# One VectorE operation in place of eight on GpSimd, a third PSUM bank for linear products, and the logarithm ahead of the exponentials, in a hybrid decoder step

## The chip, the cores and the metric

The kernel runs on one core of one Trainium2 chip. A core has engines that each work through a list of instructions of their own: TensorE (PE in the profile, with its weight loads as PEld), VectorE (DVE), ScalarE (ACT), GpSimd (POOL) and SyncE (SP), which here issues nearly all transfers. TensorE writes its products to PSUM, which this kernel uses as eight banks of 128 partitions x 512 float32 numbers; ACT and DVE read the banks out. Everything else lies in SBUF or in the chip's main memory. The metric is the device time of one execution in microseconds (us), lower is better.

## The reference

One inference step of a one-layer decoder. A group of 512 prompt tokens and a group of 8 samples with 4 new tokens each (32 tokens) go through the same weights, with model width 1024.

```python
h = _rms_norm(x, pre_mix_g)
proj = h @ w_in                       # conv value | conv gate | r | k | v | LoRA inputs | merge gates
o_a = conformer branch(proj)          # sigmoid gate, causal conv of width 31, LayerNorm, silu, w_conv_out
...
kk = k * k_k
kk = kk * lax.rsqrt(jnp.maximum(jnp.sum(kk * kk, axis=-1, keepdims=True), 1e-24))
decay = jnp.exp(-jnp.exp(w_log)); a = jax.nn.sigmoid(iclr_base + l_iclr @ w_iclr_up)
# per token and head, with a 64x64 state s:
sk = jnp.einsum('bhvk,bhk->bhv', s, kk_t)
s = s * w_t[:, :, None, :] - sk[..., None] * (kk_t * a_t)[:, :, None, :] + v_t[..., None] * k_t[:, :, None, :]
y_t = jnp.einsum('bhvk,bhk->bhv', s, r_t)
...
o_b = ((group_norm(y) + bonus) * g) @ w_rwkv_out
m = (sigmoid(gA) * o_a + sigmoid(gB) * o_b) @ w_out
x = x + _rms_norm(m, post_mix_g)
x = x + _rms_norm(jnp.square(jax.nn.relu(_rms_norm(x, pre_ffn_g) @ w_ff_up)) @ w_ff_down, post_ffn_g)
```

Outputs are the new hidden rows and the states (convolution, token shift, and the 64x64 state `s` of each of the 16 heads) of prompt and samples.

## The kernel before

Activations lie transposed: 128 channels in the partitions, the 544 tokens (512 prompt, 32 samples) in the free dimension, in two halves of 272 (or 276, with the 8 shift rows). Each float32 matrix product of a weight block is made of three products of a high and a low part (`whi`, `wlo`, `xhi`, `xlo`), L152 in `part_steps`: eight blocks of the contraction x 3 = 24 matmuls a half. Each half takes a PSUM bank with the tag `lin` from the pool `pl`, which has two; when its 24 matmuls are done, ACT or DVE or both read it out (the "evacuation"). Weights come in blocks of 128x1024: `wraw` loads one, `wsplit` makes `whi` by a copy (on ACT or POOL, L140) and `wlo` by a subtraction on DVE (L141), with two buffers for each.

The first stage, to about 830 us, computes `w_in` and the mixer for eight pairs of heads (`p` = 0 to 7). The main loop at the end of the first stage traces the work of a pair in this order: `chain(p - 1)`, which steps through the eight prompt chunks of the pair before; the block `K`; `rates(p)`; `front(p)` with the blocks `R` and `W`; `value(p)`; `tokens(p)`; the inverse of a triangular matrix for each chunk (`inverse`, 15 small steps on DVE, then products with the tag `pb`); `sample(p)`; `groupnorm(p - 1)`; and `fill`, which adds linear blocks of the gates. The `yield` statements in these generators are run through and have no effect on the order, save for the marks "R" and "front". The framework places the instructions of each engine in a fixed list when the program is built. It takes those that are ready first by the order of tracing, where its own estimate of durations says when something is ready, and gives a tile a buffer of its tag once a buffer is free. Within a list nothing overtakes. Convolution work (L292 on DVE) carries a lower priority and fills in.

PSUM in this stage: `lin` two banks, `pb` two (one tile of two banks), and one each of `aux`, `ch`, `yt` and `ax`, from the pool `qc`. `ax` serves the LoRA products and the sum over the key in `rates`, the bonus in `value`, and the group norm's products. `aux` serves `sample`. `yt` holds four chunks of the chain's output.

What the change touches:

- `rates(p)`: `sg` (decay) and `a` come from sigmoids on ACT (L458). Three exponentials of the running sum of `sg` give `pin`, `epp` and `eps` (L468 to L472). Then the key's norm: square (L477), sum by a product (L480), Ln (L481), Exp (L485). Functions of different tables need a table load on ACT (L228); `tact` (L232) keeps all such functions in the order in which they are traced.
- `sample(p)`: a small system for the 32 sample tokens in `aux`. At its end `uv` holds values in the partitions, and the new state of the eight samples is a product of `zbt` with `ux`, in which each sample's columns hold `uv` masked to that sample (L751 to L759); DVE adds the old state (L760), POOL scales it by `epS` (L762), SP stores it (L763).
- `groupnorm(p)`: mean and variance by products (L781, L784), and the gate's LoRA product (L793), in `ax`.

The second stage (from about 830 us) makes the output products and the feed-forward layers from pools of its own, `pl2` with three banks and `ql` with two, and hardly anything else.

Of the kernel before, what the change touches and what calls it, by code (L numbers as in the profile page):

```python
# [8 lines left out]
F32 = mybir.dt.float32  # L9
F32R = mybir.dt.float32r  # L10
AF = mybir.ActivationFunctionType
ALU = mybir.AluOpType
MULT, ADD, SUB = ALU.mult, ALU.add, ALU.subtract
# [4 lines left out]
NB = 8  # L18
TS = 4
N2 = T + NB * TS  # L20
N1 = N2 + NB
NPAIR = 8
C = 64
# [5 lines left out]
CDEC = math.exp(-0.5)  # L29
# [4 lines left out]
PE, ACT, DVE, SP, POOL = (getattr(mybir.EngineType, e) for e in ("PE", "Activation", "DVE", "SP", "Pool"))  # L34
# [28 lines left out]
def hybrid_step(ctx: ExitStack, tc: tile.TileContext, xT, hist, s0, win, wco, wro, wo, wup, wdn, lora,  # L63
                vecs, convw, cst, yo, convo, shifto, wkvp, wkvs):
    nc = tc.nc
    PSUM = bass.MemoryType.PSUM
    act = nc.scalar.activation
    tt, stt, ts = nc.vector.tensor_tensor, nc.vector.scalar_tensor_tensor, nc.vector.tensor_scalar
# [7 lines left out]
    pg = ctx.enter_context(tc.tile_pool(name="pg", bufs=16))  # L76
    cv = ctx.enter_context(tc.tile_pool(name="cv", bufs=1))
    wp = ctx.enter_context(tc.tile_pool(name="wp", bufs=WB))
    pl = ctx.enter_context(tc.tile_pool(name="pl", bufs=2, space=PSUM))
    dr = ctx.enter_context(tc.tile_pool(name="dr", bufs=1, space=bass.MemoryType.DRAM))  # L80

    vt = cp.tile([128, NV], F32, name="vt")
# [10 lines left out]
    rms_eps, ln_eps, gn_eps, kk_neg, kk_eps, kk_log = (epst[:, i:i + 1] for i in range(6))  # L93
# [20 lines left out]
    def con(name):  # L114
        o = COFF[name]
        return cs[:, o:o + dict(CONSTS)[name]]
# [115 lines left out]
    def tact(name, *args, **kw):  # L232

        with tables(name):
            lastact[0] = act(*args, **kw)
        return lastact[0]

    SIG, LN, EXP, LNEXP = "sigmoid_and_others", "natural_log", "exp_and_others", "natural_log_exp_and_others"
# [3 lines left out]
    with tc.tile_pool(name="p0", bufs=1) as p0, tc.tile_pool(name="q0", bufs=1, space=PSUM) as q0:  # L242
        start = tables(LNEXP)
# [8 lines left out]
        rs, rt = (p0.tile([128, N1], F32, name=n) for n in ("rs", "rt"))  # L252
        hfs = [p0.tile([128, N1], F32, name=f"hf{k}") for k in range(KT)]
        with start:
            for s, (o, m) in enumerate(S1):
                q = slice(o, o + m)
                ps = q0.tile([128, 512], F32, name=f"ss{s}")
# [21 lines left out]
    def sv(t):  # L279

        return t[:, T:N2].rearrange("p (b t) -> p b t", t=TS)
# [52 lines left out]
    with ExitStack() as c1:  # L334
# [101 lines left out]
        def sum_steps(lhsT, x, evac, pool, tag):  # L436
            for s, (o, m) in enumerate(S2):
                ps = pool.tile([128, 512], F32, name=tag, tag=tag)[:, 0:m]
                nc.tensor.matmul(ps, lhsT, x[:, o:o + m], start=True, stop=True)  # L439
                evac(s, ps, o, m)  # L440
                yield ACT

        def rates(p):

            lraw = page("k2")[:, 0:128]
            nc.sync.dma_start(lraw, lora[p, :, 0:128])
            yield (ACT,)
            glu_sig()
            yield
            for i in range(2):  # L450
                split_hl(up[0][H[i], i, :], up[1][H[i], i, :], lraw[H[i]])
            yield
            ap_ = p1.tile([128, 2 * N2], F32, name="ap", tag="ap")
            sg, a, pin = page("sg"), ap_[:, 0:N2], ap_[:, N2:2 * N2]
            for i, (d, b) in enumerate(((sg, "decay_base"), (a, "iclr_base"))):
                for s, (o, m) in enumerate(S2):
                    yield from part_steps([(up[0][:, i], up[1][:, i])], [ld], s, o, m,
                                          lambda s, ps, o, m: tact(SIG, d[:, o:o + m], ps, AF.Sigmoid, bias=vec(b, p)),  # L458
                                          qc, "ax")
            nc.vector.tensor_tensor_scan(sg[:, 0:N2], con("scan"), sg[:, 0:N2], 0.0, MULT, ADD)  # L460
            ep = p1.tile([128, NC * (C + 1) + 40], F32, name="ep")
            e0 = NC * (C + 1)
            epp = ep[:, 0:e0].rearrange("p (c t) -> p c t", c=NC)
            eps = ep[:, e0:e0 + 40].rearrange("p (b f) -> p b f", f=TS + 1)
            nc.vector.memset(epp[:, :, 0:1], 1.0)
            nc.vector.memset(eps[:, :, 0:1], 1.0)
            yield ACT
            tact(EXP, pin[:, 0:N2], sg[:, 0:N2], AF.Exp, scale=CDEC)  # L468
            yield (ACT,)
            tact(EXP, epp[:, :, 1:C + 1], ch3(sg), AF.Exp, scale=-CDEC)  # L470
            yield (ACT,)
            tact(EXP, eps[:, :, 1:TS + 1], sv(sg), AF.Exp, scale=-CDEC)  # L472
            yield ("K", p, ACT)

            k = pgs["k", p]
            k2 = page("k2")
            act(k2[:, 0:N2], k[:, 0:N2], AF.Square, scale=vec("k_k", p))  # L477
            yield
            rs = page("rs")
            yield from sum_steps(con("blk1"), k2, lambda s, ps, o, m: act(rs[:, o:o + m], ps, AF.Relu, bias=kk_neg), qc, "ax")  # L480
            tact(LN, rs[:, 0:N2], rs[:, 0:N2], AF.Ln, scale=2.0 ** 20, bias=kk_eps)  # L481
            yield (ACT,)
            kp = page("k2")
            act(kp[:, 0:N2], a[:, 0:N2], AF.Identity, scale=vec("k_a", p), bias=oka[:, p:p + 1])
            tact(EXP, rs[:, 0:N2], rs[:, 0:N2], AF.Exp, scale=-0.5, bias=kk_log)  # L485
            yield DVE
            st2(kp[:, 0:N2], k[:, 0:N2], kp[:, 0:N2], MULT)
            st2(a[:, 0:N2], a[:, 0:N2], pin[:, 0:N2], MULT)
            yield (DVE,)
            kk = page("kk")  # L490
            stt(out=kk[:, 0:N2], in0=k[:, 0:N2], scalar=vec("k_k", p), in1=rs[:, 0:N2], op0=MULT, op1=MULT)
            yield DVE
            pgs["pre"] = ep, epp, eps, a, pin, kk, kp
# [66 lines left out]
        def value(p):  # L560

            f, v, rk = fs[p], pgs["v", p], pgs["k", p]
            bon = f["bon"] = p2.tile([128, N2], F32, name="bon")
            yield from sum_steps(con("blk1"), rk, lambda s, ps, o, m: tt(out=bon[:, o:o + m], in0=ps,
                                                                       in1=v[:, 64 + o:64 + o + m], op=MULT),
                                 qc, "ax")
            if p:
                yield ("smp", p - 1, ACT)
            nc.scalar.copy(vpad[:, :, 32:64], v[:, 64 + T:64 + N2].unsqueeze(1).to_broadcast([128, 2, 32]))
            yield  # L570
# [121 lines left out]
        def sample(p):  # L692
# [55 lines left out]
            for i in range(2):  # L748
                tt(out=y[H[i], :], in0=xy[0:64, 320 + 32 * i:352 + 32 * i],
                   in1=xc[0:64, 64 * i + 32:64 * i + 64], op=ADD)  # L750
            for b in range(0, NB, 4):  # L751
                ux = p1.tile([128, 4, 64], F32, name="ux")
                for e in range(4):
                    nc.gpsimd.tensor_scalar(ux[:, e, :], uv[:, 0:64], con("bmask")[:, b + e:b + e + 1], None, MULT)  # L754
                yield
                if b == 0:
                    ps = qc.tile([128, NB, 64], F32, name="aux", tag="aux")
                nc.tensor.matmul(ps[:, b:b + 4].rearrange("p b v -> p (b v)"), zbt, ux.rearrange("p b v -> p (b v)"),
                                 start=True, stop=True)  # L759
            tt(out=st, in0=ps, in1=st, op=ADD)  # L760
            for b in range(NB):
                nc.gpsimd.tensor_scalar(st[:, b, :], st[:, b, :], f["epS"][:, b:b + 1], None, MULT)  # L762
# [3 lines left out]
        def groupnorm(p):  # L766
            f, y = fs[p], pgs["y", p]
            nc.scalar.copy(y[:, T:N2], ys[p])
            yc, sq = page("t0", cv), page("t1", cv)
            lraw = yc[:, 0:128]  # L770
            nc.sync.dma_start(lraw, lora[p, :, 128:256])
            lhi = p1.tile([128, 128], F32R, name="lhi")
            llo = p1.tile([128, 128], F32R, name="llo")
            yield ACT
            split_hl(lhi, llo, lraw)
            yield

            def cevac(s, ps, o, m):
                act(sq[:, o:o + m], ps, AF.Square)
                nc.scalar.copy(yc[:, o:o + m], ps)  # L780
            yield from sum_steps(con("cent"), y, cevac, qc, "ax")  # L781
            yield
            rs = sq
            yield from sum_steps(con("blkm"), sq,  # L784
                                 lambda s, ps, o, m: tact(LNEXP, rs[:, o:o + m], ps, AF.Ln, bias=gn_eps), qc, "ax")
            tact(LNEXP, rs[:, 0:N2], rs[:, 0:N2], AF.Exp, scale=-0.5)
            yield DVE
            o = yc[:, 0:N2]
            stt(out=o, in0=o, scalar=vec("lnx_g", p), in1=rs[:, 0:N2], op0=MULT, op1=MULT)
            yield DVE  # L790
            stt(out=o, in0=f["bon"], scalar=vec("lnx_b", p), in1=o, op0=ADD, op1=ADD)
            yield
            for s, (oo, m) in enumerate(S2):  # L793
                yield from part_steps([(lhi, llo)], [lg], s, oo, m,
                                      lambda s, ps, oo, m: tt(out=yc[:, oo:oo + m], in0=ps, in1=yc[:, oo:oo + m], op=MULT),
                                      qc, "ax")
            nc.sync.dma_start(o_dr[p], o)

        def block(b, p):
# [110 lines left out]
    for j in range(KT):  # L910
        o = page("o")
# [235 lines left out]
```

## Time and profile before

| | us |
|---|---|
| median of 3 runs | 1377.77 (1374.94 to 1379.05) |
| the profiled execution | 1375.78 |
| its span, first to last instruction | 1373.6 |
| mean granted TensorE clock | 0.963 |

"Busy" is the time in which an engine executed something; matmuls overlap each other, so PE busy is not PE at its peak. The windows give this per stretch of time. A wait is an idle time of an engine before an instruction, with the instruction of another engine that ended it ("PE lin L152 <- DVE r L379": PE stood before a linear product until DVE's evacuation at line 379 was done). "issue" is idle time that the profile ties to nothing. In a timeline, a row gives start, duration, engine, line and tiles (output<-inputs), and in brackets the idle time ahead of it. In groups of instructions the columns are count, busy us, mean ns of one, and the idle us before them.

### The profile page before, as it was taken

The numbers are of one execution on the slowest core, as the hardware profiler recorded it, in microseconds if no ns is written. First come the engines' busy times: TensorE is split into PE (matmuls) and PEld (weight loads), VectorE is DVE, ScalarE is ACT, GpSimd is POOL, SyncE is SP. The second block draws the span as 40 slices with busy tenths as digits, with TensorE's granted clock in tenths as the row PEclk, the third lists the DMA queues.
The fourth block names the chain that finished last, engine by engine and source line by source line (L and its number), as shares of the span: only waits on it lengthen the run. The fifth ranks groups of instructions, "written<-read, shape, count | busy, mean of one in ns | idle before, by whom it ended". The sixth has DMA issues, their size and how long they took to land.

```text
span 1373.6 us, 23314 instructions
## 1 busy us (share of the span) xinstructions
PE 1266.3 (92%) x9170; PEld 1192.4 (87%) x9170; DVE 811.7 (59%) x1521; ACT 672.5 (49%) x1595; POOL 245.5 (18%) x376
## 2 busy tenths in 40 slices
PE   6978998989899798898889999999999999999996
PEld 5968887787787778778788999999999999999995
DVE  5798768653876768767657746566833221333345
ACT  7452746657374563743733438245755322555231
POOL 2125333142433225232230120000000000000000
PEclk9999998999999899999999999999999999999998
DMA  5312111111201212012121565245023222322331
GB/s 183 99 46 90 45 47 48 30 65 34 77 18 42 77 34 64 31 42 87 33 65 44 177 215 173 89 128 177 28 62 93 86 84 83 101 81 91 93 93 66
DMA packets 46333, 110.61 MB, mean 81 GB/s; under 512 B 7184, under 2 KB 17680, under 8 KB 46224
## 3 DMA queue, kind: packets, MB, share of 16 engines
q1 hardware_dynamic: 46080, 109.05, 25.0%
q8 instruction: 72, 1.18, 0.3%
q14 instruction: 37, 0.30, 0.1%
q10 hardware_dynamic: 144, 0.07, 0.0%
HBM read 94.79 MB, written 14.32 MB: 79 GB/s over the span
## 4 chain that ended last, share of the span: by engine, by line
PE 64%; ACT 9%; DVE 7%; POOL 4%; issue 3%; DMA 1%; SPq 0%; DVEq 0%; POOLq 0%; ACTq 0%
PE lin L152 47%; PE pb L608 4%; ACT SV L679 2%; PE ax L439 2%; POOL ux L754 2%; POOL st L762 2%; PE ch L664 2%; PE ch L675 2%; ACT SV L673 2%; PE ch L671 1%; PE ax L152 1%; DVE c L292 1%; PE yt L668 1%; PE pb L544 1%; PE ch L666 1%
## 5 line engine op out<-in xcount | busy, mean ns | idle before, releaser
L152 PE MATMUL lin<-xh,whi 128*128 128x272 f32 (+1 forms) x2096 | 623.8, 298 | 22.1 <-DVE r L379 10.3
L152 PE MATMUL lin<-xh,wlo 128*128 128x272 f32 (+1 forms) x2096 | 624.5, 298 | 0.6 <-DVE wlo L141 0.6
L152 PE MATMUL lin<-xl,whi 128*128 128x272 f32 (+1 forms) x2096 | 622.4, 297 | 0.1
L152 PEld LDWEIGHTS lin<-xh,whi 128*128 128x128 f32 x2096 | 405.4, 194 | 25.7 <-issue 13.6
L152 PEld LDWEIGHTS lin<-xh,wlo 128*128 128x128 f32 x2096 | 405.0, 193 | 1.9 <-DVE wlo L141 0.8
L152 PEld LDWEIGHTS lin<-xl,whi 128*128 128x128 f32 x2096 | 404.6, 193 | 1.3 <-DVE xl L174 0.3
L141 DVE TENSOR_TENSOR wlo<-raw,whi 128x1024 fp32r<-128x1024 f32 x131 | 160.6, 1226 | 211.1 <-ACT whi L140 175.9
L292 DVE SCALAR_TENSOR_TENSOR c<-u,cw,c 128x512 f32<-128x512 f32 x240 | 187.0, 779 | 8.9 <-issue 4.8
L140 ACT CAST whi<-raw 128x1024 fp32r<-128x1024 f32 x76 | 79.7, 1049 | 122.4 <-PE lin L152 118.8
L140 POOL CAST whi<-raw 128x1024 fp32r<-128x1024 f32 x55 | 65.3, 1187 | 314.6 <-issue 166.0
L152 PE MATMUL lin<-xh,wl 128*128 128x272 f32 x240 | 69.4, 289 | 0.0
L152 PE MATMUL lin<-xl,wh 128*128 128x272 f32 x240 | 69.3, 289 | 0.0
L152 PE MATMUL lin<-xh,wh 128*128 128x272 f32 x240 | 69.2, 288 | 0.0
L1006 DVE TENSOR_TENSOR xl<-ff,xh 128x272 fp32r<-128x272 f32 x64 | 28.3, 442 | 55.9 <-ACT ff L1005 55.9
L228 ACT ACT_TABLE_LOAD x45 | 57.7, 1283 | 2.0 <-PEq L1129 1.2
L679 ACT ACTIVATE SV<-ch,pc 64x64 f32<-64x64 f32 x128 | 39.5, 309 | 20.4 <-PE ch L675 19.1
L673 ACT ACTIVATE SV<-ch 64x64 f32<-64x64 f32 x128 | 27.9, 218 | 37.0 <-PE ch L671 35.1
L152 PEld LDWEIGHTS lin<-xh,wh 128*128 128x128 f32 x240 | 45.2, 188 | 0.1
L152 PEld LDWEIGHTS lin<-xh,wl 128*128 128x128 f32 x240 | 45.2, 188 | 0.1
L152 PEld LDWEIGHTS lin<-xl,wh 128*128 128x128 f32 x240 | 45.1, 188 | 0.1
L754 POOL TENSOR_SCALAR ux<-uv,cs 128x64 f32<-128x64 f32 x64 | 33.9, 549 | 51.6 <-DVE uv L745 47.2
L762 POOL TENSOR_SCALAR st<-st,epS 128x64 f32<-128x64 f32 x64 | 40.0, 648 | 11.4 <-DVE rt L588 5.8
(275 smaller groups left out, 1894.1 us busy)
## 6 DMA issues: line engine op xcount, KB each, us to landing
raw<-win SPq DMA_DIRECT2D x58, 512.0 KB, 3.6
raw<-wup SPq DMA_DIRECT2D x32, 512.0 KB, 3.6
raw<-wdn SPq DMA_DIRECT2D x32, 512.0 KB, 3.6
g_dr<-g SPq DMA_DIRECT2D x16, 272.0 KB, 2.3
raw<-wro SPq DMA_DIRECT2D x8, 512.0 KB, 3.9
raw<-wco SPq DMA_DIRECT2D x8, 512.0 KB, 3.6
raw<-wo SPq DMA_DIRECT2D x8, 512.0 KB, 3.6
x<-xT SPq DMA_DIRECT2D x8, 276.0 KB, 5.0
```

Source lines behind the costliest of these rows:

```text
L140: upper(hi, r)
L141: tt(out=lo, in0=r, in1=hi.bitcast(F32), op=SUB)
L152: nc.tensor.matmul(ps, a, b[:, o:o + m], start=k == 0 and i == 0, stop=k == n - 1 and i == 2)
L228: lastact[0] = nc.scalar.preload_act_table_set(name)
L292: stt(out=c[:, 0:T], in0=u[:, t:t + T], scalar=w[:, t:t + 1], in1=c[:, 0:T], op0=MULT, op1=ADD)
L439: nc.tensor.matmul(ps, lhsT, x[:, o:o + m], start=True, stop=True)
L608: nc.tensor.matmul(ps[:, c, :], lhsT(c), rhs[:, c, :], start=True, stop=True)
L673: nc.scalar.mul(SV[H[i], c, i, :], ch[H[i], 2, B[i]], -1.0)
L679: nc.scalar.mul(SV[H[i], c + 1, i, :], ch[H[i], 1, B[i]], pc[H[i], c:c + 1])
L754: nc.gpsimd.tensor_scalar(ux[:, e, :], uv[:, 0:64], con("bmask")[:, b + e:b + e + 1], None, MULT)
L762: nc.gpsimd.tensor_scalar(st[:, b, :], st[:, b, :], f["epS"][:, b:b + 1], None, MULT)
L1006: tt(out=lo[:, q], in0=t[:, q], in1=hi[:, q].bitcast(F32), op=SUB)
```

## The change

Four edits.

1. In `sample`, the eight POOL operations that masked `uv` for each sample, in two groups of four with a product of 256 columns each, become one `tensor_tensor` on DVE with both operands broadcast (128 x 8 x 64 = 512 columns) and one product of 512 columns.
2. The pool `pl` for linear products has three banks in place of two.
3. The bank `ax` is gone: `rates` and `value` now take theirs from `aux`, which `sample` uses too, and `groupnorm` takes its from `yt`, which the chain uses.
4. In `rates`, the three exponentials of the decay stand behind the Ln and the Exp of the key's norm.

```diff
-    pl = ctx.enter_context(tc.tile_pool(name="pl", bufs=2, space=PSUM))
+    pl = ctx.enter_context(tc.tile_pool(name="pl", bufs=3, space=PSUM))
...
                                           lambda s, ps, o, m: tact(SIG, d[:, o:o + m], ps, AF.Sigmoid, bias=vec(b, p)),
-                                          qc, "ax")
+                                          qc, "aux")
...
-            yield ACT
-            tact(EXP, pin[:, 0:N2], sg[:, 0:N2], AF.Exp, scale=CDEC)
-            yield (ACT,)
-            tact(EXP, epp[:, :, 1:C + 1], ch3(sg), AF.Exp, scale=-CDEC)
-            yield (ACT,)
-            tact(EXP, eps[:, :, 1:TS + 1], sv(sg), AF.Exp, scale=-CDEC)
-            yield ("K", p, ACT)
...
-            yield from sum_steps(con("blk1"), k2, lambda s, ps, o, m: act(rs[:, o:o + m], ps, AF.Relu, bias=kk_neg), qc, "ax")
+            yield from sum_steps(con("blk1"), k2, lambda s, ps, o, m: act(rs[:, o:o + m], ps, AF.Relu, bias=kk_neg), qc, "aux")
             tact(LN, rs[:, 0:N2], rs[:, 0:N2], AF.Ln, scale=2.0 ** 20, bias=kk_eps)
...
             tact(EXP, rs[:, 0:N2], rs[:, 0:N2], AF.Exp, scale=-0.5, bias=kk_log)
+            tact(EXP, pin[:, 0:N2], sg[:, 0:N2], AF.Exp, scale=CDEC)
+            tact(EXP, epp[:, :, 1:C + 1], ch3(sg), AF.Exp, scale=-CDEC)
+            tact(EXP, eps[:, :, 1:TS + 1], sv(sg), AF.Exp, scale=-CDEC)
...
-            for b in range(0, NB, 4):
-                ux = p1.tile([128, 4, 64], F32, name="ux")
-                for e in range(4):
-                    nc.gpsimd.tensor_scalar(ux[:, e, :], uv[:, 0:64], con("bmask")[:, b + e:b + e + 1], None, MULT)
-                yield
-                if b == 0:
-                    ps = qc.tile([128, NB, 64], F32, name="aux", tag="aux")
-                nc.tensor.matmul(ps[:, b:b + 4].rearrange("p b v -> p (b v)"), zbt, ux.rearrange("p b v -> p (b v)"),
-                                 start=True, stop=True)
+            ux = p1.tile([128, NB, 64], F32, name="ux")
+            tt(out=ux, in0=uv[:, 0:64].unsqueeze(1).to_broadcast([128, NB, 64]),
+               in1=con("bmask").unsqueeze(2).to_broadcast([128, NB, 64]), op=MULT)
+            ps = qc.tile([128, NB, 64], F32, name="aux", tag="aux")
+            nc.tensor.matmul(ps.rearrange("p b v -> p (b v)"), zbt, ux.rearrange("p b v -> p (b v)"), start=True, stop=True)
             tt(out=st, in0=ps, in1=st, op=ADD)
...
```

In `value` the last argument `"ax"` becomes `"aux"`, and in the three places of `groupnorm` it becomes `"yt"`.

More of the change, by code (lines that the diff above doesn't have):

```diff
@@ L565, in value @@
                                                                        in1=v[:, 64 + o:64 + o + m], op=MULT),
-                                 qc, "ax")
+                                 qc, "aux")
             if p:
@@ L780, in cevac @@
                 nc.scalar.copy(yc[:, o:o + m], ps)
-            yield from sum_steps(con("cent"), y, cevac, qc, "ax")
+            yield from sum_steps(con("cent"), y, cevac, qc, "yt")
             yield
@@ L784, in groupnorm @@
             yield from sum_steps(con("blkm"), sq,
-                                 lambda s, ps, o, m: tact(LNEXP, rs[:, o:o + m], ps, AF.Ln, bias=gn_eps), qc, "ax")
+                                 lambda s, ps, o, m: tact(LNEXP, rs[:, o:o + m], ps, AF.Ln, bias=gn_eps), qc, "yt")
             tact(LNEXP, rs[:, 0:N2], rs[:, 0:N2], AF.Exp, scale=-0.5)
@@ L795, in groupnorm @@
                                       lambda s, ps, oo, m: tt(out=yc[:, oo:oo + m], in0=ps, in1=yc[:, oo:oo + m], op=MULT),
-                                      qc, "ax")
+                                      qc, "yt")
             nc.sync.dma_start(o_dr[p], o)
```

## The prediction

> **What bounds the kernel now.** I read the page first (engines, slices, clock), then the windows, then PE's waits in order of size, then the groups and the timelines around the three places that the change touches.
>
> ```profile
> span 1373.6 us, 23314 instructions
> PE 1266.3 (92%) x9170; PEld 1192.4 (87%) x9170; DVE 811.7 (59%) x1521; ACT 672.5 (49%) x1595; POOL 245.5 (18%) x376
> PEclk9999998999999899999999999999999999999998
> 200.00:460.00 260.00, 229.44 (x1534) 204.41 (x1533) 177.93 (x370) 144.33 (x389) 82.97 (x130) 0.94 0.16 51
> 830.00:1373.60 543.60, 528.63 (x4186) 526.04 (x4185) 234.19 (x406) 239.57 (x456) 0.00 (x0) 0.99 0.30 93
> ```
>
> The last two rows are windows: start:end, length, then busy us of PE, PEld, DVE, ACT, POOL, then the granted clock. After 830 us PE is busy for 528.6 of 543.6 us at clock 0.99, and POOL not at all. The change touches nothing there. In 200:460, three pairs of the mixer, PE idles 30.6 us and the clock is 0.94, so of 260 us some 15.6 us more go to half clock: a mean of 0.94 with states 1.00 and 0.50 (below) is 31 us at half. This is what a reordering can win: at most about 46 us in 260, so some 95 us in the 530 us from 200 to 730. PE's own work does not shrink. So the question is which of PE's waits the change removes.
>
> ```profile
> PE aux L758 <- POOL ux L754: 18.6, 14, 2.9
> PE lin L152 <- DVE r L379: 10.3, 4, 6.6
> PE pb L608 <- ACT nw L601: 9.6, 7, 4.0
> PE lin L152 <- DVE t L379: 3.8, 1, 3.8
> PE ch L671 <- ACT xs L667: 3.7, 3, 1.3
> PE lin L152 <- DVE rt L588: 3.2, 1, 3.2
> PE lin L152 <- DVE R L590: 2.7, 1, 2.7
> PE lin L152 <- ACT g L330: 1.3, 2, 1.0
> PE aux L747 <- DVE uv L745: 0.2, 1, 0.2
> ```
>
> PE's waits: total us, times, longest. The largest is the very product that the change rewrites.
>
> **Part 1, samples' values spread on DVE.** Removed: 64 POOL operations (eight a pair), with one wait of PE for each group of four. Added: eight DVE operations of 128x512. The two matmuls a pair of 256 columns become one of 512, the same columns.
>
> ```profile
> L754 POOL TENSOR_SCALAR ux<-uv,cs 128x64 f32<-128x64 f32 x64 | 33.9, 549 | 51.6 <-DVE uv L745 47.2 <-PE aux L758 2.8 <-ACT c L289 1.6
> L622 DVE TENSOR_TENSOR nw<-D,pb 128x512 f32<-128x512 f32 x16 | 11.0, 687 | 31.4 <-PE pb L608 31.4
> L292 DVE SCALAR_TENSOR_TENSOR c<-u,cw,c 128x512 f32<-128x512 f32 x240 | 187.0, 779 | 8.9 <-issue 4.8
> L564 DVE TENSOR_TENSOR bon<-ax,v 128x272 f32<-128x272 f32 x16 | 7.0, 437 | 18.5 <-PE ax L439 18.4
> ```
>
> POOL loses 33.9 us. DVE gains 8 x 0.69 = 5.5 us (row L622, the same size), which its 82 idle us of 260 take in. No row has two spread operands at that size: from below I bound one by the 0.44 us of 272 columns (L564), from above by twice L622, 1.4 us, and take 0.69, the row of its own size. The new product waits for `uv`, then one DVE operation. The nearest row for such a wait is L747, the product just before it, which waits for DVE's `uv`: 0.2 us in all eight pairs. From the other side, one convolution step (0.78) may stand ahead of the new operation each time: 6.2 us. I take 2, nearer to L747, since both neighbours are DVE work in the same short sequence. Gain 18.6 - 2 = **16.6** (12.4 to 18.4).
>
> Then POOL's list: the weight casts behind `ux` move up, but the scaling of `st` (L762), which also waits for this product, inherits the wait at the head. DVE's `st` sum no longer waits through two rounds. SP issues the store of `st` and, behind it, the load of the next LoRA block, so both come some 3 us sooner. I count nothing for these: they sit beside PE's work.
>
> There is a second price to those stalls: the granted clock.
>
> ```profile
> 114.50:121.30 6.80, 6.10 (x25) 5.92 (x26) 5.26 (x15) 0.39 (x1) 4.91 (x8) 0.50 0.25 77
> 277.50:280.40 2.90, 0.38 (x4) 0.15 (x3) 1.51 (x3) 0.00 (x0) 2.84 (x6) 1.00 0.46 133
> 281.70:285.10 3.40, 3.40 (x18) 3.40 (x17) 2.15 (x12) 0.00 (x0) 3.20 (x8) 0.50 0.03 12
> 353.40:356.80 3.40, 3.28 (x12) 3.10 (x13) 1.47 (x5) 0.00 (x0) 2.49 (x6) 0.50 0.00 0
> 705.00:711.80 6.80, 5.88 (x24) 5.38 (x23) 3.12 (x14) 0.32 (x1) 4.43 (x11) 0.50 0.29 96
> 452.00:455.00 3.00, 0.29 (x3) 0.14 (x2) 3.00 (x8) 0.00 (x0) 0.86 (x1) 1.00 0.52 175
> 455.80:462.60 6.80, 5.28 (x24) 4.98 (x23) 6.76 (x13) 4.48 (x12) 2.99 (x4) 0.50 0.24 75
> 565.00:571.80 6.80, 5.94 (x27) 5.94 (x27) 6.77 (x13) 3.04 (x10) 5.84 (x8) 0.50 0.29 88
> ```
>
> Windows with the same columns. From 277.5 to 280.4 PE does 0.38 us of work, standing at L758, and from 281.7 the clock is 0.50. Four such stretches follow `ux` stalls (6.8, 3.4, 3.4, 6.8: 20.4 us), and each us at half clock loses half: 10.2 us at most, nothing at least if another idle stretch brings the half clock anyway. I take **5**.
>
> The Trainium skill, "TensorE: Matmul & The Clock Gate", section "What's actually happening", says the array falls to half clock after an idle window of about 3.4 us and returns after a busy one. By that rule a stall under 3 us should not do it, and the clock terms here would be nothing. The trace speaks against it: 2.5 to 2.9 us nearly idle came before 281.7, though not wholly without work.
>
> **Part 2, a third bank for the linear products.** The bank that a linear half-block filled is free only after ACT and DVE have read it. When DVE is late, PE stands.
>
> ```profile
> L152 PE MATMUL lin<-xh,whi 128*128 128x272 f32 (+1 forms) x2096 | 623.8, 298 | 22.1 <-DVE r L379 10.3 <-DVE t L379 3.8 <-DVE rt L588 3.2
> 73.89 1.22 DVE L141 TENSOR_TENSOR wlo<-raw,whi 128x1024 fp32r<-128x1024 f32 x1
> 77.01 0.57 PE L152 MATMUL lin<-xh,whi 128*128 128x276 f32 x1 [6.61 <-DVE r L379]
> ```
>
> 22.1 us of waits stand before first matmuls of linear groups. The one by `t` (3.8) is at the start, where the operands are only just split: not counted. The longest (6.61, before 77.01) would give some 2, since the next block's `wlo` is ready only at 75.11. The others are 3.7 of `r`, 3.2, 2.7 and 1.3: 10.9, as DVE stands in the inverse's steps while an evacuation queues behind them. A third bank lets PE run one half-block on: 24 matmuls at a pitch of 543.6 / 4186 = 0.13 us are 3.1 us, as long as these stalls. Together 13; bounds 0 (no split weights at hand: there are still two weight buffers) and 18.3. I take **10**. Of the half-clock stretches at 455.8 and 565.0 behind such stalls (13.6 us, 6.8 lost) I take **3**.
>
> **Part 3, the logarithm ahead of the exponentials.** One table load a pair goes: sigmoid, Ln, Exp instead of sigmoid, Exp, Ln, Exp.
>
> ```profile
> L228 ACT ACT_TABLE_LOAD x45 | 57.7, 1283 | 2.0 <-PEq L1129 1.2
> 299.41 1.28 ACT L228 ACT_TABLE_LOAD   x1
> 300.70 0.66 ACT L235 ACTIVATE ap<-sg 128x544 f32<-128x544 f32 x1
> 301.27 0.73 ACT L235 ACTIVATE ep<-sg 128x512 f32<-128x512 f32 x2
> 302.39 1.28 ACT L228 ACT_TABLE_LOAD   x1
> 303.69 0.45 ACT L673 ACTIVATE SV<-ch 64x64 f32<-64x64 f32 x2
> ```
>
> 8 x 1.28 = 10.3 us of ACT in a stretch without gaps, and the key's norm comes another 0.66 + 0.73 earlier, as three exponentials now follow it. They then delay what DVE needs of `pin` and `epp`, by at most 8 x 1.39 = 11.1. PE's waits for ACT in that stretch (L671, 3.7) are small. So between 10.3 won and 11.1 less 10.3 = 0.8 lost; I take **3**, nearer to the waits that PE shows.
>
> The skill's "ScalarE: Activation LUTs", section "What ACT_TABLE_LOAD costs", adds about 1.38 us of drain to 1.28 for each switch; by that the part would take 8 x 2.66 = 21.3 us off ACT and I would take 6. The trace disagrees: the load ends at 303.67 and the next operation starts at 303.69.
>
> **Part 4, one bank shared.** Front and samples take turns in `aux`, the group norm joins `yt`.
>
> ```profile
> 257.50 0.33 PE L696 MATMUL aux<-ar,zbk 128*128 128x64 f32 x2
> 276.55 0.43 DVE L795 TENSOR_TENSOR t<-ax,t 128x272 f32<-128x272 f32 x1
> 277.21 0.39 PE L668 MATMUL yt<-LR,SV 128*128 128x128 f32 x2
> 281.11 0.69 DVE L760 TENSOR_TENSOR st<-aux,st 128x512 f32<-128x512 f32 x1 [2.10 <-PE aux L758]
> 288.30 0.28 PE L152 MATMUL ax<-xh,uph 128*128 128x272 f32 x1
> ```
>
> The norm's last reading ends at 276.98 and the chain's first `yt` starts at 277.21. The samples let go of `aux` at 281.80, and the next pair's rates first need it at 288.30. So the two would take turns already: **0**, with 6.5 us of cover. If the cover is gone, see the second rival.
>
> **The sum.** 16.6 + 5 + 10 + 3 + 3 = 37.6 us. A stall that goes is partly paid at the next: after the samples, PE comes to the products of the inverse (L608 waits 9.6 us for ACT's `nw`, seven times), whose chain on DVE is not shortened. I take a third off, by judgement; the size is that of L608's wait beside it and the samples' own, 9.6 of 9.6 + 18.6. That leaves 37.6 x 2/3 = 25.1 us. The profiled execution took 1375.78 us, 2.2 over its span; 1375.8 - 25.1 = 1350.7. The median of the three runs is 1377.77, 2.0 higher, so **1353**.
>
> **The rivals.**
>
> *The stalls only move.* PE reaches L608 and the chain's links sooner and waits there; the third bank finds no split weights. Then part 1 alone counts, with half given back: some 8 us, about 1369, or nothing at all. For it: L608's 9.6 us directly behind. Against it: linear work stands between in every pair.
>
> *The shared bank turns against it* (slower). With a third bank linear work is planned denser, and the rates' first product may be placed before the samples are through. The samples hold `aux` from 257.50 to 281.80, so PE, at the head of its list, would stand until DVE's `st` sum. It decides from the point where the rates come 6.5 us earlier than now against the samples. Its price is about 6 us in seven pairs, 42 us, less the 25: 17 slower, 1395. Against it: the samples get some 3 us shorter.
>
> *No clock gain.* Half clock comes from other idle stretches too, so the 8 us of clock fall away: 29.6 x 2/3 = 20, 1358. This is also the skill's rule on the clock gate.
>
> *More.* All terms near their upper ends, 18.4 + 10.2 + 18.3 + 6.8 + 10.3 = 64, without giving back a third: down to 1314.
>
> **How the numbers follow.** Forecast 0.45 (1336 to 1366 around 1353), no clock gain 0.10, more 0.10, stalls move with 4 to 14 us left 0.12, stalls move with nothing left 0.09, slower 0.14. A measurement of this kernel tells about 0.3%, 4 us, from no change. Faster by more: 0.45 + 0.10 + 0.10 + 0.12 = 0.77; the same 0.09; slower 0.14. The range 1328 to 1381 leaves out about half of "more" and most of "slower", 0.05 + 0.13.
>
> **What would show it.** Right: L754 gone from POOL and at some 0.69 us x8 on DVE; PE's wait at the samples' last product under 3 us in all; waits of `lin` for L379, L588, L590 under 10; 37 table loads; granted clock in 200:460 above 0.95; after 830 us nothing shorter or longer but its start. Wrong: `aux` or `yt` products waiting for L760 or for a bank's reader; L608's wait well above 10 us; `lin` waiting for `wlo`; a new place of half clock. The prediction falls if the order on PE differs so much that the chain or the inverse comes late by more than the removed waits.

## The result: 1329.1 us, and the profile after

The changed kernel takes 1329.1 us (median of four runs, 1327.13 to 1342.23) against 1376.36 before (four runs, 1374.7 to 1379.05): a ratio of 0.9672, 95% interval 0.9616 to 0.9728, 47.3 us less. The forecast was 1353, some 25 us less, with 1328 as the lower end of its range. The profiled execution happens to be the slowest of the changed kernel's: 1342.23 us.

These are rows of the changed kernel's page: the span, the busy times, the granted clock by slice.

```profile
span 1340.4 us, 23228 instructions
...
PE 1263.0 (94%) x9154; PEld 1189.1 (89%) x9154; DVE 814.7 (61%) x1529; ACT 661.2 (49%) x1587; POOL 200.2 (15%) x312
...
PEclk9999989979799898999989999999999999999998
```

PE's idle time, the span less PE's busy time, was 1373.6 - 1266.3 = 107.3 us and is 1340.4 - 1263.0 = 77.4: 29.9 less, of 33.2 us by which the span is shorter. PE's busy time hardly moved, 1266.3 to 1263.0, and it holds the half clock too. POOL lost 45 us and ACT 11.

The next two fences are windows of the kernel before and of the changed one: start:end, length, then busy us of PE, PEld, DVE, ACT, POOL, and the granted clock. The first row of each covers the same length at the end of the span.

```profile
820.00:1373.60 553.60, 538.63 (x4266) 536.04 (x4265) 237.30 (x409) 245.40 (x465) 0.00 (x0) 0.99 0.31 97
60.00:730.00 670.00, 592.50 (x3965) 531.14 (x3963) 474.11 (x944) 357.30 (x953) 219.10 (x332) 0.93 0.16 51
```

```profile
786.80:1340.40 553.60, 536.04 (x4231) 533.23 (x4229) 236.11 (x408) 242.55 (x460) 0.00 (x0) 0.99 0.30 94
60.00:730.00 670.00, 620.21 (x4188) 555.07 (x4187) 504.46 (x993) 364.01 (x998) 179.02 (x270) 0.95 0.18 55
200.00:460.00 260.00, 241.17 (x1589) 215.47 (x1589) 182.38 (x365) 146.49 (x395) 68.17 (x104) 0.92 0.16 49
350.60:356.20 5.60, 0.22 (x2) 0.00 (x0) 5.60 (x13) 2.63 (x7) 1.05 (x2) 0.84 0.00 0
356.20:363.00 6.80, 6.74 (x31) 6.77 (x32) 4.22 (x6) 2.87 (x6) 2.75 (x4) 0.50 0.26 77
```

The last 553.6 us of both hold nearly the same PE work (538.6 and 536.0 us): the second stage is what it was. So the gain lies in the first stage, most of which is the mixer, where 670 us now hold 620 us of PE's work in place of 592, at a clock of 0.95 in place of 0.93. The last two rows show what is left: PE does 0.22 us of work in 5.6, and 6.8 us at half clock follow.

PE's waits in the changed kernel (total us, times, longest), and then its groups of instructions:

```profile
PE pb L604 <- ACT nw L597: 29.8, 8, 6.0
...
PE ch L660 <- ACT SV L675: 2.3, 8, 0.8
PE lin L152 <- DVE g L910: 1.9, 1, 1.9
...
PE ch L671 <- ACT SV L669: 1.5, 6, 0.3
```

```profile
L152 PE MATMUL lin<-xh,whi 128*128 128x272 f32 (+1 forms) x2096 | 618.9, 296 | 3.4 <-DVE g L910 1.9
L754 POOL TENSOR_SCALAR st<-st,epS 128x64 f32<-128x64 f32 x64 | 40.6, 657 | 11.3 <-DVE rt L584 9.5 <-DVE R L586 1.8
L751 PE MATMUL aux<-ux,zbt 128*128 128x512 f32 x16 | 8.7, 625 | 1.6 <-DVE rt L584 0.7 <-DVE R L586 0.4
L748 DVE TENSOR_TENSOR ux<-uv,cs 128x512 f32<-128x512 f32 x8 | 5.5, 684 | 0.0
L228 ACT ACT_TABLE_LOAD x37 | 47.5, 1283 | 1.8 <-PEq L1121 1.2
```

The lines have moved: L604 here is L608 before, L751 is L758, L660 is L664, L671 is L675, and L754 is now the scaling of the state, which was L762. The wait at the samples' product went from 18.6 to 1.6 us, the waits at the linear products' first matmul from 22.1 to 3.4, and eight table loads are gone. One wait grew, the one ahead of the inverse's products: 9.6 to 29.8.

### The profile page after: what moved, and what is told of

Same layout as the page of the kernel before. It is cut to its first block, busy times and chain, and to the rows that moved or that the text cites. A ratio compares the mean times of both kernels' runs of the same rounds, so it can differ in the third digit from the quotient of the medians.

```text
span 1340.4 us, 23228 instructions
## 1 busy us (share of the span) xinstructions
PE 1263.0 (94%) x9154; PEld 1189.1 (89%) x9154; DVE 814.7 (61%) x1529; ACT 661.2 (49%) x1587; POOL 200.2 (15%) x312
## 4 chain that ended last, share of the span: by engine, by line
PE 67%; DVE 12%; ACT 11%; issue 3%; DMA 3%; POOL 3%; SPq 0%; DVEq 0%; ACTq 0%; POOLq 0%
PE lin L152 48%; PE pb L604 6%; DVE c L292 2%; ACT SV L675 2%; POOL st L754 2%; ACT SV L669 1%; DVE wlo L141 1%; PE ch L671 1%; PE yt L439 1%; PE ch L660 1%; PE ch L667 1%; PE pb L540 1%; DMA raw<-wup 1%; PE aux L720 1%; DVE R L586 1%
## 5 line engine op out<-in xcount | busy, mean ns | idle before, releaser
L152 PE MATMUL lin<-xh,wlo 128*128 128x272 f32 (+1 forms) x2096 | 618.1, 295 | 0.6 <-DVE wlo L141 0.6
L152 PEld LDWEIGHTS lin<-xh,whi 128*128 128x128 f32 x2096 | 400.8, 191 | 5.7 <-DVE g L910 2.2
L292 DVE SCALAR_TENSOR_TENSOR c<-u,cw,c 128x512 f32<-128x512 f32 x240 | 186.9, 779 | 3.9 <-DVE c L292 0.4
L140 POOL CAST whi<-raw 128x1024 fp32r<-128x1024 f32 x55 | 62.2, 1130 | 302.6 <-PE lin L152 173.8
L604 PE MATMUL pb<-nw,NQ 128*128 128x64 f32 x128 | 25.5, 383 | 29.8 <-ACT nw L597 29.8
L604 PEld LDWEIGHTS pb<-nw,NQ 128*128 128x128 f32 x128 | 24.3, 292 | 31.3 <-issue 31.3
L675 ACT ACTIVATE SV<-ch,pc 64x64 f32<-64x64 f32 x128 | 39.5, 309 | 15.2 <-PE ch L671 13.7
L754 POOL TENSOR_SCALAR st<-st,epS 128x64 f32<-128x64 f32 x64 | 40.6, 657 | 11.3 <-DVE rt L584 9.5
```

The costliest lines, as they stand in the source:

```text
L140: upper(hi, r)
L152: nc.tensor.matmul(ps, a, b[:, o:o + m], start=k == 0 and i == 0, stop=k == n - 1 and i == 2)
L292: stt(out=c[:, 0:T], in0=u[:, t:t + T], scalar=w[:, t:t + 1], in1=c[:, 0:T], op0=MULT, op1=ADD)
L604: nc.tensor.matmul(ps[:, c, :], lhsT(c), rhs[:, c, :], start=True, stop=True)
L675: nc.scalar.mul(SV[H[i], c + 1, i, :], ch[H[i], 1, B[i]], pc[H[i], c:c + 1])
```

## The experiments

All on the same kind of chip, each beside runs of the kernel before; the ratio is to those. Edits are numbered as in the section on the change. "Mean clock" is the mean over the runs of that kernel; for the kernel before it is taken over the 28 runs beside e1 to e13, and the 11 beside e14 would make it 0.964.

| kernel | median us | ratio to before, 95% | mean clock |
|---|---|---|---|
| before | 1377.0 | | 0.965 |
| the change | 1329.1 | 0.9672 (0.9616 to 0.9728) | 0.973 |
| edit 1 alone (e1_ux) | 1358.82 | 0.9865 (0.9823 to 0.9908) | 0.966 |
| edits 2 and 3 (e2_bank) | 1348.18 | 0.9792 (0.9761 to 0.9824) | 0.972 |
| edit 4 alone (e3_log) | 1370.33 | 0.9947 (0.9928 to 0.9966) | 0.967 |
| edit 3 alone (e4_share) | 1378.22 | 1.001 (0.9994 to 1.0026) | 0.965 |
| edits 1, 3, 4 (e6_no_bank) | 1352.92 | 0.9831 (0.981 to 0.9852) | 0.968 |
| the change, state scaled on DVE (e8_scale_dve) | 1304.87 | 0.95 (0.945 to 0.9549) | 0.985 |
| the change, two buffers of `st` (e9_two_st) | 1328.51 | 0.9653 (0.9634 to 0.9672) | 0.974 |
| e8 and e9 together (e10_both) | 1302.15 | 0.9455 (0.9431 to 0.948) | 0.988 |
| before, state scaled on DVE (e11_before_scale) | 1357.84 | 0.9868 (0.9826 to 0.991) | 0.971 |
| e10, LoRA load early (e12_lora) | 1303.17 | 0.9471 (0.9416 to 0.9526) | 0.985 |
| e10, two linear banks (e13_two_banks) | 1326.47 | 0.9657 (0.9613 to 0.97) | 0.978 |
| the change, LoRA load early (e14_lora_alone) | 1324.2 | 0.9628 (0.9594 to 0.9663) | 0.975 |

### The edits one by one

Edit 2 can't stand alone, since all eight banks were taken before: it goes with edit 3, and edit 3 is run alone beside it.

```diff
e1_ux: the kernel before with this
-            for b in range(0, NB, 4):
-                ux = p1.tile([128, 4, 64], F32, name="ux")
...
+            tt(out=ux, in0=uv[:, 0:64].unsqueeze(1).to_broadcast([128, NB, 64]),
+               in1=con("bmask").unsqueeze(2).to_broadcast([128, NB, 64]), op=MULT)
...
e2_bank: the kernel before with this, and "ax" -> "aux" or "yt"; e4_share: the names alone
-    pl = ctx.enter_context(tc.tile_pool(name="pl", bufs=2, space=PSUM))
+    pl = ctx.enter_context(tc.tile_pool(name="pl", bufs=3, space=PSUM))
e3_log: the kernel before with the three exponentials (L468 to L472) moved behind L485
```

> Only the samples' values spread by one DVE operation (edit 1); two linear banks, ax kept, exponentials first. Theory A, the sum of the prediction: 16.6 + 5 less a third, 14 us faster (8 to 25), PE's wait at the last sample product under 3 us, the linear waits on L379, L588, L590 still near 20 us. Theory B, the third bank carries most of the 47 us: 10 us faster or less. Theory C, no part has a price of its own because each edit makes a new order of the lists: anything, but the single edits do not add up to 47 within 10 us.

> Only edits 2 and 3: third linear bank, ax merged into aux and yt; POOL spreads the samples' values as before. Theory A: 9 us faster (0 to 20), linear waits on L379, L588, L590 under 10 us, the wait at the samples' product still near 18 us. Theory B: 25 to 40 us faster. Theory C as above.

> Only edit 4: logarithm ahead of the exponentials; 37 table loads. Theory A: 2 us faster (10 faster to 1 slower). Theory B: within 3 us. Theory C: up to 10 us either way.

> Only edit 3: ax merged into aux and yt, still two linear banks, one bank left unused. Theory A: no change within 4 us, since the two took turns already. Rival: the shared bank holds up the rates, 4 to 20 us slower, with waits of aux products on L760 or of yt products on L795.

Measured against 1376.91 us before: 18.1 us less for edit 1, 28.7 less for edits 2 and 3, 6.6 less for edit 4, and 1.3 more for edit 3 alone, whose interval holds no change. So the bank comes out as Theory B had it (25 to 40) and not as the forecast's own term (0 to 20), and the sum of the single edits stays within the 10 us of 47 beyond which Theory C would have held. PE's waits with edit 1 alone, then with edits 2 and 3:

```profile
PE pb L608 <- ACT nw L601: 21.7, 7, 4.1
PE lin L152 <- DVE r L379: 7.9, 3, 6.6
...
PE aux L755 <- DVE R L590: 1.9, 2, 1.2
```

```profile
PE pb L608 <- ACT nw L601: 22.1, 8, 5.6
PE aux L758 <- POOL ux L754: 19.3, 15, 3.0
...
PE lin L152 <- DVE r L379: 4.3, 2, 3.5
...
PE ch L664 <- ACT SV L679: 2.6, 9, 0.5
...
PE ch L675 <- ACT SV L673: 1.3, 5, 0.4
```

And the rows of the kernel before that stand against the last two:

```profile
PE ch L675 <- ACT SV L673: 5.5, 13, 0.6
...
PE ch L664 <- ACT SV L679: 3.8, 11, 0.7
PE ch L671 <- ACT xs L667: 3.7, 3, 1.3
PE ax L152 <- ACT sg L235: 3.5, 2, 2.0
```

With edit 1 the wait for POOL is gone and 12 us of it come back ahead of the inverse's products (9.6 to 21.7). With the bank the waits of the linear products shrink, and so do those of the chain, whose products are not in that bank at all: L675 from 5.5 to 1.3, L664 from 3.8 to 2.6, L671 from 3.7 to nothing among the larger waits, and the rates' first product from 3.5 (`ax`) to 1.0 (`aux`). That PE has linear work at hand while the chain's next link is being read out is the likely reason; the rows show the shorter waits and not what fills them. PE's idle time falls from 107.3 to 1341.0 - 1252.5 = 88.5 us, and the mean clock rises from 0.965 to 0.972. In this profile, too, 12 us come back at L608 (9.6 to 22.1).

The single gains add up to 18.1 + 28.7 + 6.6 = 53.4 us, against 47.3 for the whole change.

### The change without the bank

```diff
-    pl = ctx.enter_context(tc.tile_pool(name="pl", bufs=3, space=PSUM))
+    pl = ctx.enter_context(tc.tile_pool(name="pl", bufs=2, space=PSUM))
```

> The changed kernel with two linear banks again (edits 1, 3 and 4 without 2; one PSUM bank unused). The single edits measured 18, 29 and 7 us faster than before. Theory A, terms that add: 18 + 7 faster than before, so about 1352, with the linear waits on DVE evacuations back near 20 us. Theory B, the third bank is what makes the other edits pay (they cover each other's stalls): within 8 us of before. Rival: shared bank without the third costs on top, slower than 1365.

1352.92 us, 24.1 less than before: edits 1, 3 and 4 add up (18.1 + 6.6 - 1.3 = 23.4) and give nothing back among themselves. The bank on top is worth 1352.92 - 1329.1 = 23.8, against 28.7 alone. So some 5 us seem to be given back between the bank and the other edits. The intervals don't tell them from none: by its own, the bank's 28.7 is anything from 24 to 33.

### The wait that grew

The 29.8 us ahead of L604 were the next question. The chain of waits of the changed kernel around the longest but one of them (start, us, what):

```profile
335.52 0.60 DVE st L752
336.12 0.12 DVE R L586
336.24 5.64 POOL st L754 x8
341.89 2.24 DMA wkvs<-st
344.35 1.05 POOL whi L140
345.42 1.23 DVE wlo L141
...
347.33 1.03 DVE R L586
...
356.26 3.65 PE pb L604 x16
```

POOL scales the new state in eight operations, 5.64 us. In this pair its list then holds a memset of the same buffer, which waits for the store of the state, and only then the cast of a weight block. DVE's subtraction `wlo` waits for that cast, and the steps of the inverse stand behind `wlo` in DVE's list. Among these steps, in the rows left out, the same chain holds 3.1 us of convolution (L292, L299, L301), a part of the delay that no run took out. PE runs dry for 5.44 us, and L604 comes late. Three edits to the changed kernel:

```diff
e8_scale_dve
-            for b in range(NB):
-                nc.gpsimd.tensor_scalar(st[:, b, :], st[:, b, :], f["epS"][:, b:b + 1], None, MULT)
+            tt(out=st, in0=st, in1=f["epS"].unsqueeze(2).to_broadcast([128, NB, 64]), op=MULT)
e9_two_st
-            sx = p1.tile([128, NB + 1, 64], F32, name="st")
+            sx = p1.tile([128, NB + 1, 64], F32, name="st", bufs=2)
e10_both: both
```

> The changed kernel, in which the eight POOL operations that scale the new sample state (some 5.5 us a pair) become one DVE operation with a broadcast scale (0.69 us). Theory P: the wait that grew, PE's first product of the inverse on ACT's copy (29.8 us), comes from POOL: scale, store, memset, weight cast, then DVE's subtraction and the inverse's steps behind it. Then that wait falls below 15 us and the time by 10 to 25 us against the changed kernel (1305 to 1320). Rival D: the inverse is late because of convolution steps between its own on DVE; then the wait stays above 25 us and the time within 5 us.

> The changed kernel with two buffers for the sample state, so that the memset of the next one (and the weight cast behind it on POOL) need not wait for the store. Theory P: POOL's wait for the store (some 2.3 us a pair) goes, a gain of 3 to 12 us. Rival D: within 4 us.

> The changed kernel with both: scaling on DVE and two buffers for the sample state. Theory P: 12 to 30 us faster than the changed kernel, so 1300 to 1317, the wait of the inverse's first product below 12 us, granted clock above 0.98. Rival D: within 6 us.

With the scaling on DVE the time falls by another 24.2 us, to 1304.87, and this group and this wait stand in its profile:

```profile
L753 DVE TENSOR_TENSOR st<-st,epS 128x512 f32<-128x512 f32 x8 | 5.4, 681 | 0.0
```

```profile
PE pb L604 <- ACT nw L597: 9.1, 7, 2.5
```

40.6 us of POOL became 5.4 us of DVE, and the wait ahead of L604 is back at the 9 us that it had before the change. PE's idle time is 1295.7 - 1237.0 = 58.7 us. The second buffer brought nothing (1328.51), but it did not take away what it was meant to take: POOL still waits 10.6 us in six times for the store, against 14.0 in seven, since the framework now places the memset of a later pair behind the store. So e9 doesn't tell what that wait costs. What speaks against a price is e10, where POOL waits 13.0 us for the same store in three longer waits, and which has the lowest median of all.

Was that price there before the change?

> The kernel before, with the samples' state scaled by one DVE operation and nothing else of the change. Theory P1: the eight POOL scalings cost as much before as after (they hold up the weight cast, the inverse and so PE): 15 to 25 us faster than before. Theory P2: before the change the stalls at the samples' product and at the linear banks covered that delay (the wait at the inverse's first product was only 9.6 us): 0 to 8 us faster, so the price only came to light with the change.

It was. The same line put into the kernel before gives 1357.84, 20.7 us less than the 1378.56 beside it. But it was paid elsewhere. The wait ahead of L608 hardly moves (9.6 to 8.9). The rows of `lin` among PE's waits fall from 22.6 us in all to 15.4, PE's idle time falls from 107.3 to 97.1, and the mean clock rises from 0.965 to 0.971. DVE's wait for POOL's casts shrinks with it, in the kernel before and then with the scaling on DVE:

```profile
DVE wlo L141 <- POOL whi L140: 34.8, 16, 3.8
```

```profile
DVE wlo L141 <- POOL whi L140: 14.1, 8, 3.7
```

And the chain of the kernel before had said so, in a row that the prediction did not read, the shares of the span by line:

```profile
by line: PE lin L152 47.2%; PE pb L608 4.2%; issue 3.3%; ACT SV L679 2.1%; PE ax L439 1.8%; POOL ux L754 1.7%; POOL st L762 1.6%; PE ch L664 1.6%; PE ch L675 1.6%; ACT SV L673 1.5%; PE ch L671 1.2%; PE ax L152 0.9%; DVE c L292 0.9%; PE yt L
```

1.6% of 1373.6 us are 22 us at `st` L762, beside 1.7%, 23 us, at `ux` L754: the measured prices are 20.7 and 18.1. In the changed kernel the share at the scaling is 2.1%, 28 us, for a measured 24.2. The shares point at the right lines; that 22 came so near to 20.7 is within the noise. PE never waits for L762 itself, so it stands in none of PE's waits.

### By which road the scaling is paid

The load of the group norm's LoRA block stands behind the store of the state in SP's list, and ACT waits in its list for that load (10.1 us with the scaling on DVE); in the changed kernel:

```profile
ACT lhi L173 <- DMA t<-lora: 27.5, 8, 5.6
```

So a second road leads from the scaling to `nw`, over ACT. Followed back from L604 pair by pair, the chain of the changed kernel takes this second road in four of the eight pairs, which hold 18.5 of the 29.8 us. It goes through the cast and `wlo`, as above, in two (9.1 us), and in one (1.5 us) from the scaling to another operation in POOL's list. One of the four:

```profile
498.31 5.36 POOL st L754 x8
503.68 2.20 DMA wkvs<-st
506.37 3.35 DMA t<-lora
509.75 0.31 ACT lhi L173
...
516.10 3.65 PE pb L604 x16
```

Two runs load the block ahead of the samples into a buffer of its own, on e10 and on the change itself.

```diff
-            lraw = yc[:, 0:128]
-            nc.sync.dma_start(lraw, lora[p, :, 128:256])
+            lraw = lraws[p]
...
+                lraws[p] = p2.tile([128, 128], F32, name="lraw")
+                nc.sync.dma_start(lraws[p], lora[p, :, 128:256])
                 run(sample(p))
```

> Scaling on DVE and two state buffers on top of the changed kernel, and the group norm's LoRA block loaded into a buffer of its own ahead of the samples, so that ACT's cast no longer stands behind that load. If the load is what still holds the inverse's copies on ACT: 3 to 8 us faster than without, near 1297. If it is hidden: within 3 us of 1302.

> The changed kernel with one edit: the group norm's LoRA block is loaded into a buffer of its own ahead of the samples, so that it no longer queues on SP behind the store of the scaled state; GpSimd still scales the state. In the changed kernel ScalarE stands 27.5 us in 8 waits at the split of that block (lhi) for the load; with VectorE's scaling 10.1 us in 6. Theory A, the scaling's price goes through the late LoRA load and ScalarE's list: most of the 24 us is won here too, 1305 to 1313. Theory B, it goes through GpSimd's list, whose weight cast stands behind the eight scalings and holds VectorE at the low part of the weights: ScalarE's wait for the load goes, and the time stays, 1325 to 1333. In between: both roads end at the same products, and each alone wins a part.

On e10 it brings nothing (1303.17 against 1302.15): with the scaling on DVE the load has no price that these runs could tell. On the change it gives 1324.2, 4.9 us less than 1329.1, with intervals that overlap. ACT's wait for the load is gone there, and these remain, DVE's wait for POOL's casts and PE's ahead of L604:

```profile
DVE wlo L141 <- POOL whi L140: 39.2, 17, 4.4
```

```profile
PE pb L604 <- ACT nw L597: 24.6, 8, 5.5
```

The chain moves with it: in e14 it goes from the scaling through the cast and `wlo` in five of the eight pairs, which hold 21.9 of the 24.6 us. So the two roads run nearly level. With the load out of the way the other one holds PE almost as long, and the load's road alone is worth some 5 us; the spread of the runs leaves anything from nothing to some 14. The scaling stands at the head of both, and its edit takes both away. No run had only the casts moved, so what the road through POOL's list is worth by itself is not shown.

A new order of the lists as such is a rival to any of these gains. e4, e9 and e12 also give the framework something else to place, and each lies within 1.3 us of the kernel that it edits, which speaks against it.

### The bank once more

> Scaling on DVE and two state buffers on top of the changed kernel, but with two linear banks. The third bank was worth 24 us in the changed kernel and 29 us alone. If it is worth that because it gives PE linear work between the chain's links: again 20 to 30 us, so 1322 to 1332. If it was mainly the cover for POOL's delay, which is gone here: under 12 us, 1302 to 1314.

1326.47 with two linear banks against 1302.15 with three: 24.3 us, as in the change (23.8). PE's waits with two banks and then with three, both with the scaling on DVE:

```profile
PE ch L660 <- ACT SV L675: 5.4, 12, 1.2
PE ch L671 <- ACT SV L669: 3.9, 9, 1.2
```

```profile
PE ch L660 <- ACT SV L675: 2.9, 11, 0.5
...
PE ch L671 <- ACT SV L669: 1.9, 8, 0.4
```

These links of the chain wait half as long, and the mean clock is 0.988 against 0.978. Over the whole list the larger part lies ahead of the linear products themselves: the rows of `lin` add up to 14.6 us with two banks and 4.0 with three, those of `ch` to 12.0 and 8.9. So the bank doesn't need POOL's delay in order to pay; that the chain's pauses are its main worth is not shown. e10 beats both kernels: 27 us below the change, 75 below the kernel before. Whether it is better than e8 (1304.87) can't be told from these runs.

## Why the prediction was right, and where its sizes failed

The direction and the mechanism were right, and the time lies in the range, but only just: 1.1 us inside its fast end, with almost twice the gain of the forecast. Point by point:

**Part 1**, 16.6 of idle time and 5 of clock, 21.6: measured 18.1 for the edit alone (13 to 24 by its interval). The residual wait of 2 us was 1.6, the duration of 0.69 us was 0.684. As a sum the term held, and that was in part luck. In e1 PE's idle time fell by 12.3 us (107.3 to 95.0) and not by 16.6, since 12 of the 18.6 came back at L608 and smaller waits that the term didn't count shrank elsewhere.

**Part 2** is the term that was mis-sized: 10 of idle time and 3 of clock, 13, where 28.7 were measured (24 on top of other edits). To part the two, take the time times one less the mean clock as an estimate of what half clock costs. Over the runs it is 48.9 us before and 37.4 with the bank (32.2 to 41.9 in single runs). By this some 11.5 us are clock, where 3 were put down with 6.8 as the most, and 17 are idle time, where 10 were put down with 18.3 as the most. So the step that failed is the size of the clock term, and behind it a count that looked only at the waits ahead of linear products. In e2's profile these fall by 16.8 us (the rows of `lin` add up to 22.6 before and 5.8 with the bank). The chain's waits, which were not counted, fall by 10.8 (16.1 to 5.3), and 12.5 come back at L608.

**Part 3**, 3: measured 6.6 (5 to 10 by its interval), half way between the value taken and the upper bound of 10.3. The eight loads went as counted. The rows of DVE's waits in e3 hold 0.2 us for the later exponentials, where up to 11.1 had been feared.

**Part 4**, 0: measured +1.3, not to be told from no change. The rival of a shared bank that turns against it did not appear; no product of `aux` or `yt` waits for a bank's reader by more than 0.5 us in e2; in e4 the longest such wait is 1.8 us, of `aux` for `bon`, and before it was 1.5 on `ax`.

**The third that was taken off** failed as well. Of the 53.4 us of the single edits a third would have been 18; 6.1 were given back, a ninth, and the intervals (some 11 us on that difference, an estimate) don't tell this from nothing. Most of what comes back at L608 does so within a single edit already, 12 us in e1 and in e2 each. The mechanism was seen rightly in its place, L608's wait, and that was the sign named for a wrong prediction: it rose to 29.8. But the reason was not the one given, a chain of inverse steps on DVE that isn't shortened: with POOL's scaling gone it is 9.1. And other waits shrank by more than it grew, so PE's idle time still fell by 29.9 us.

**"They sit beside PE's work"**, said of POOL's list and of the stores behind it, is the sentence that was wrong outright. The scaling of the state cost 20.7 us before the change and costs 24.2 after it.

**The rivals.** "Stalls only move" and "slower" are out at 47 us. Of "no clock gain": the clock part falls from 48.9 to 35.4 us (means over all runs), so by that estimate 13.5 us of the 45 us by which the means differ are clock, and the forecast had 8 of 37.6. The rule of the Trainium skill behind that rival ("TensorE: Matmul & The Clock Gate", section "What's actually happening", half clock after an idle window of about 3.4 us) would fit the changed kernel's longest stalls, 5.6 us with 0.22 of work; but these windows of e10 go against it:

```profile
483.50:486.00 2.50, 0.03 (x1) 0.02 (x1) 2.50 (x6) 1.72 (x5) 0.81 (x1) 0.98 0.00 0
486.00:492.80 6.80, 6.79 (x32) 6.80 (x32) 4.40 (x5) 3.75 (x9) 2.46 (x4) 0.50 0.23 77
```

2.5 us with 0.03 of work, and half clock after, so a shorter stall than the rule's window was enough here. The sign "clock in 200:460 above 0.95" did not come in the profiled execution (0.92), which was the slowest; its own stalls ahead of L604 are the place of half clock that the signs spoke of.

## What to carry to other kernels

Read the chain's shares by line for every engine before calling an engine's work hidden: a line can be in nobody's waits on the main engine and still hold 1.6% of the chain. For the three lines tried here the share came within 5 us of the measured price (22, 23 and 28 us for 20.7, 18.1 and 24.2). One more accumulation bank can be worth more than the waits ahead of its own products: here half-clock time and the waits of a dependent chain beside it shrank too. Where a slow engine's list mixes small element work with casts and stores that others wait for, one broadcast operation on a faster engine with room can pay several times its own length. And where two roads lead from one cause to the same wait, taking away one shows little: look for what heads both.

## What was not expected of the hardware

Executions of one program can differ almost by their clock alone. The changed kernel took 1327.13 us at a mean clock of 0.977 and 1342.23 at 0.966. Time times one less the clock is 30.5 and 45.6 us: the difference, 15.1, is the whole difference of the times. e8's fastest and slowest run differ by 14.1 us (1297.49 at 0.990, 1311.55 at 0.981), of which this makes 11.9, and e8's mean clocks fell into two groups in its four runs, 0.99 and 0.98, for the same program. It does not hold for every kernel: the kernel before took 1372.81 us at 0.965 and 1379.24 at 0.967. Half clock was seen behind stalls of 2.5 to 5.6 us, in the windows above; which stalls it follows in which execution is not shown, as each kernel has one profile.
